# Two kinds of tile for the attention's matmuls, and a reversal done by reads, in a two-layer hybrid block

## The chip, the cores and the metric

The kernel runs on one core of one Trainium2 chip. Its engines are TensorE (PE, with its weight loads as PEld), VectorE (DVE), ScalarE (ACT), GpSimd (POOL) and SyncE (SP), whose queue issues most of the DMA transfers. The metric is device microseconds of one execution.

## What is computed

The reference runs two layers over 256 latent tokens and 256 context tokens of width 1024. A layer is a half-step SwiGLU, then four token mixers side by side (a 31-tap convolution, a gated linear recurrence in both directions, a gated delta net in both directions, and attention with 8 query heads over 2 key heads of width 64), merged through gates, projected, and a second half-step SwiGLU. The second layer computes no context output. Cut to what the change touches:

```python
# attention: keys in the window (latent tokens) and all context keys; a sink per head
s = einsum('bqhgd,bkhd->bhgqk', qg, kk) * 64 ** -0.5        # masked to the band
probs = softmax(concatenate(logits + [sink_col], -1))
out = einsum('bhgqk,bkhd->bqhgd', probs[..., :n], vv)        # the sink's share is dropped
...
# delta net: one direction runs on reversed tokens, its output is reversed back
o = o_forward + flip(o_backward)
y = o * rsqrt(mean(o * o) + eps) * g_norm * silu(z)
```

## The kernel before

All arithmetic is float32. The large matmuls split each operand into two float32r parts (lines 120 and 121 make the parts of a weight, on ACT and on POOL or DVE) and add three products (lines 379 to 381). Tokens lie in four tiles of 128: tiles 0 and 1 are the context, 2 and 3 the latent tokens; the second layer's mixer works on tiles 2 and 3 alone.

The mixer's streams are written as generators, and a hand-written string of letters (ORDER, one for each layer) says in which order their pieces are emitted: "a" is one step of the attention's scores, "b" one of its values, "g" the delta net, "s" its scan, "l" the recurrence, "c" the convolution, "z" gates, "m" merges. A second string (TAIL) orders the delta net's output ("o"), the last merges and the output projection. The framework then schedules the pieces onto the engines by priority, with a timeline of its own estimates (schedule_with_timeline_sim in build), so the order on an engine follows from the dependencies and the free buffers as well as from the letters. SBUF units of 128×512 come from pools (T has 6, G has 8), PSUM banks from three (pm 3, pg 3, px 2).

A step of the attention is one token tile t and one group g: two query heads, one for each key head, stacked on the 128 partitions (64 each). There are 16 steps in the first layer (8 with 256 keys for the context, 8 with 512 for the latent tokens) and 8 of 512 keys in the second. Before, att_z makes two copies of the keys, each with the other head's 64 partitions set to zero (line 1173). att_scores multiplies the stacked queries with each copy over all 128 partitions (line 1210), adds the band's mask by a matmul for latent tokens (line 1213), takes the maximum (line 1214) and the exponential with its sum (line 1221); the sink's exponential, the sum and its reciprocal follow (lines 1223 to 1225). The scores of a context step share one px bank, those of a latent step take two. att_values transposes the unnormalised probabilities (line 1241), copies them back to SBUF (line 1242), multiplies them as stationary operand with 64 columns of values (line 1247), so that tokens lie on the partitions, and scales by the reciprocal (line 1250). After the fourth group the tile is transposed (line 1255), copied (line 1257) and written out (line 1258).

gdn_out, called for four tiles in the first layer and for two in the second, reads a tile of each direction's output from DRAM (line 959) and the gate (line 961), reverses the tokens of the second by a matmul with the matrix J (line 964), which reverses each block of 32, adds both (line 966), squares (line 969), normalises and transposes (line 978). The scan's output lies in DRAM as [pair of chunks, 128, direction, 256], where the 128 are 4 heads by 32 tokens.

Of the kernel before, what the change touches and what calls it, by code (L numbers as in the profile page):

```python
# [17 lines left out]
P = 128  # L18
# [31 lines left out]
class Net:  # L50
# [482 lines left out]
        else:  # L533
            nc.vector.tensor_add(x, x, t1)

# [1 line left out]

    def z_mm(self, ps, w, H, c):
        for k in range(KD):
# [413 lines left out]
    def gdn_out(self, go, y):  # L953
        nc = self.nc
        V = nc.vector
        o1, ot, sz = self.G(), self.G(), self.G()
        tok = slice(go * P, (go + 1) * P)
        for x, d, g in ((o1, 1, (1 - go) if go < 2 else (5 - go)), (ot, 0, go)):
            nc.sync.dma_start(x.rearrange("p (q c) -> p q c", q=2),
                              self.ospill[2 * g:2 * g + 2, :, d].rearrange("q p c -> p q c"))  # L960
        nc.sync.dma_start(sz.rearrange("p (h t) -> p h t", h=4), self.szspill[:, :, tok])
        pj = self.ps("pg")
        for i in range(4):
            nc.tensor.matmul(pj[:, (3 - i) * P:(4 - i) * P], self.gcst("J"), o1[:, i * P:(i + 1) * P],
                             start=True, stop=True)
        V.tensor_add(ot, pj, ot)
        sq = self.small(4, "osq", 1)
        for i in range(4):
            nc.scalar.activation(pj[:, i * P:(i + 1) * P], ot[:, i * P:(i + 1) * P], AF.Square,
                                 accum_out=sq[:, i:i + 1])  # L970
        V.tensor_scalar(sq, sq, 1.0 / 128, 4 * NORM_EPS, op0=ALU.mult, op1=ALU.add)
        rr = self.small(4, "orr", 1)
        nc.gpsimd.tensor_tensor(rr, sq, self.mhalf[:, :4], op=ALU.pow)
        o3 = ot.rearrange("p (n e) -> p n e", n=4)
        V.tensor_mul(o3, o3, rr.unsqueeze(2).to_broadcast([P, 4, P]))
        pt = self.ps("pg")
        for i in range(4):
            nc.tensor.transpose(pt[:, i * P:(i + 1) * P], ot[:, i * P:(i + 1) * P], self.ident)
        p4 = pt.rearrange("p (n h t) -> p n h t", n=4, h=4)
        for h in range(4):  # L980
            y3 = o1[:, h * P:(h + 1) * P].rearrange("p (n t) -> p n t", n=4)
            V.scalar_tensor_tensor(y3, p4[:, :, h], self.vec[:, V_GN:V_GN + 1],
                                   sz[:, h * P:(h + 1) * P].rearrange("p (n t) -> p n t", n=4),
                                   op0=ALU.mult, op1=ALU.mult)
        self.y_part(y, tok, o1.rearrange("p (h t) -> p h t", h=4))
# [152 lines left out]
    def att_z(self, l, H, last):  # L1138
# [24 lines left out]
        def k():  # L1163
            load()
            S["kv"] = self.slot("B", name="kv")
            u = [S["kv"][:, e * 512:(e + 1) * 512] for e in range(4)]
            kf = u[3]
            S["vt"] = u[2]
            rope(self.z(l, Z_AK, H, full), full, kf)
            S["kz"] = []  # L1170
            for i in range(2):
                kk = u[i]
                V.tensor_scalar(kk, kf, S["ac"][:, 896 + i:897 + i], None, op0=ALU.mult)
                S["kz"].append(kk)

        def v():
            pv = self.z(l, Z_AV, H, full)
# [20 lines left out]
    def att_scores(self, S, t, g):  # L1198
# [4 lines left out]
        q = S["q"][:, g * 512 + t * P:g * 512 + (t + 1) * P]  # L1203
        w = (4 if t >= 2 else 2) * P
        mx, den, es = (self.small(2, n, 3) for n in ("mx", "den", "es"))
        ps = [self.ps("px") for _ in range(w // 256)]
        if t < 2:
            ps = [ps[0][:, :w], ps[0][:, w:]]
        for kv in range(2):
            nc.tensor.matmul(ps[kv], q, S["kz"][kv][:, :w], start=True, stop=t < 2)  # L1210
            if t >= 2:
                o = 5 - t
                nc.tensor.matmul(ps[kv][:, o * P:(o + 1) * P], self.ident, band[t - 2], start=False, stop=True)
            V.reduce_max(mx[:, kv:kv + 1], ps[kv], axis=mybir.AxisListType.X)
# [8 lines left out]
        nc.scalar.activation(es, es, AF.Exp)  # L1223
        V.tensor_add(den, den, es)
        V.reciprocal(den, den)
        S["pr"].append((pr, den))

    def att_values(self, S, t, g):
        nc = self.nc
        V = nc.vector  # L1230
        pr, den = S["pr"].pop(0)
        nk = 4 if t >= 2 else 2
        w = nk * P
        if g == 0:
# [6 lines left out]
                nc.tensor.transpose(pt[kv][:, kt * P:(kt + 1) * P], pr[kv][:, kt * P:(kt + 1) * P], self.ident)  # L1241
            nc.scalar.copy(pr[kv], pt[kv])
        po = self.ps("px")
        for kv in range(2):
            o = po[:, 64 * kv:64 * kv + 64]
            for kt in range(nk):
                nc.tensor.matmul(o, pr[kv][:, kt * P:(kt + 1) * P],
                                 S["vt"][:, kt * P + 64 * kv:kt * P + 64 * kv + 64],
                                 start=kt == 0, stop=kt == nk - 1)
        V.tensor_mul(S["ya"][:, g * P:(g + 1) * P].rearrange("p (k e) -> p k e", k=2),  # L1250
                     po[:, :P].rearrange("p (k e) -> p k e", k=2), den.unsqueeze(2).to_broadcast([P, 2, 64]))
        if g == 3:
            pt = self.ps("px")
            for e in range(4):
                nc.tensor.transpose(pt[:, e * P:(e + 1) * P], S["ya"][:, e * P:(e + 1) * P], self.ident)
            yt = self.T()
            nc.scalar.copy(yt, pt)
            nc.sync.dma_start(self.ysp[3][:, :, t * P:(t + 1) * P], yt.rearrange("p (g t) -> p g t", g=4))

    def y_split(self, b, c):  # L1260
        y = self.new_y()
# [297 lines left out]
```

## Time and profile before

| | us |
|---|---|
| median of 3 runs | 2820.98 (2819.75 to 2821.17) |
| span of the profiled execution | 2816.3 |
| the median above that span | 4.7 |
| PE busy | 2593.8 |
| DVE busy | 1955.0 |
| ACT busy | 1093.3 |
| POOL busy | 1008.0 |

The profile is of one execution; its span runs from the first to the last instruction that it shows, and what lies around the span is in the runs' times alone. PE's busy time counts each matmul with its modelled end, so instructions overlap in it; what an instruction costs in a row of them is read from start to start.

### The profile page before, as it was taken

How to read it: one execution, taken by the hardware profiler on the slowest of the kernel's cores; microseconds unless marked ns; L12 is line 12 of the kernel's file. 1: busy time of each engine (PE TensorE's matmuls, PEld its weight loads, DVE VectorE, ACT ScalarE, POOL GpSimd, SP SyncE). 2: the span in 40 equal slices, each digit the busy share in tenths (PEclk: the TensorE clock that was granted, in tenths of full speed). 3: DMA queues.
4: the chain of work that ended last, by engine and by line, in shares of the span. 5: the costliest groups of instructions: out<-in, count | busy, mean ns of one | idle time of the engine just before them, and what ended most of it. 6: DMA issues, size and time to landing. Idle time of an engine off the chain costs nothing.

```text
span 2816.3 us, 37869 instructions
## 1 busy us (share of the span) xinstructions
PE 2593.8 (92%) x14382; PEld 2174.2 (77%) x14382; DVE 1955.0 (69%) x3129; ACT 1093.3 (39%) x1995; POOL 1008.0 (36%) x691
## 2 busy tenths in 40 slices
PE   5999998998898999999999999999979878888898
PEld 3787877776777787878878888888867767688898
DVE  8695966678999834265969467623698898756455
ACT  3322235483332533353222442223536534344443
POOL 4323223222535344433232332323332278731221
PEclk9999999999999999999999999999989989999899
DMA  6554542234422343434545344423222534357353
GB/s 226 191 179 169 201 145 102 69 109 153 140 83 91 113 135 117 164 113 157 181 171 196 102 166 167 149 95 115 91 90 92 156 116 133 105 183 240 135 181 118
DMA packets 162216, 396.99 MB, mean 141 GB/s; under 512 B 28417, under 2 KB 68577, under 8 KB 161265
## 3 DMA queue, kind: packets, MB, share of 16 engines
q1 hardware_dynamic: 158114, 384.55, 40.9%
q10 hardware_dynamic: 3888, 9.96, 1.1%
q8 instruction: 113, 1.85, 0.3%
q14 instruction: 69, 0.57, 0.1%
q0 software_dynamic: 32, 0.07, 0.0%
HBM read 360.92 MB, written 33.60 MB: 140 GB/s over the span
## 4 chain that ended last, share of the span: by engine, by line
PE 34%; DVE 13%; issue 3%; DMA 2%; POOL 2%; ACT 2%; SPq 0%; POOLq 0%; ACTq 0%; DVEq 0%
PE pm L380 10%; PE pm L381 10%; PE pm L379 10%; DVE C L1107 2%; DVE G L572 1%; DVE junk L169 1%; DVE wl L121 1%; DVE G L864 1%; PE px L381 1%; PE px L380 1%; PE px L379 1%; DMA wr<-in_wo_dram 1%; DVE lru L1049 1%; DVE M L781 1%; PE pg L873 0%
## 5 line engine op out<-in xcount | busy, mean ns | idle before, releaser
L379 PE MATMUL pm<-h,wh 128*128 128x512 f32 (+1 forms) x2512 | 895.5, 358 | 36.6 <-ACT h L125 12.8
L381 PE MATMUL pm<-h,wl 128*128 128x512 f32 (+1 forms) x2512 | 890.9, 355 | 16.8 <-DVE wl L121 14.8
L380 PE MATMUL pm<-h,wh 128*128 128x512 f32 (+1 forms) x2512 | 892.0, 355 | 13.0 <-POOL h L127 6.7
L121 POOL TENSOR_TENSOR wl<-wr,wh 128x1024 fp32r<-128x1024 f32 x166 | 419.8, 2530 | 697.6 <-ACT wh L120 649.0
L120 ACT CAST wh<-wr 128x1024 fp32r<-128x1024 f32 x340 | 356.7, 1050 | 785.6 <-PE pm L380 275.2
L379 PEld LDWEIGHTS pm<-h,wh 128*128 128x128 f32 x2512 | 484.0, 193 | 109.1 <-ACT h L125 15.6
L381 PEld LDWEIGHTS pm<-h,wl 128*128 128x128 f32 x2512 | 484.8, 193 | 87.0 <-DVE wl L121 18.8
L380 PEld LDWEIGHTS pm<-h,wh 128*128 128x128 f32 x2512 | 485.1, 193 | 80.9 <-POOL h L127 10.1
L121 DVE TENSOR_TENSOR wl<-wr,wh 128x1024 fp32r<-128x1024 f32 x174 | 243.6, 1400 | 263.0 <-ACT wh L120 261.6
L169 DVE SCALAR_TENSOR_TENSOR junk<-wa,cb 128x1024 bf16<-128x1024 f32 x256 | 358.3, 1442 | 9.2 <-DMA wa<-in_adaw_dram 8.6
L127 POOL TENSOR_TENSOR F<-G,F 128x512 fp32r<-128x512 f32 (+1 forms) x94 | 139.4, 1483 | 426.2 <-ACT F L125 426.1
L1107 DVE SCALAR_TENSOR_TENSOR C<-C,vec 128x482 f32<-128x482 f32 (+29 forms) x240 | 208.2, 867 | 4.1 <-ACT C L1099 0.9
L380 PE MATMUL pm<-wl,F 128*128 128x512 f32 x368 | 145.5, 395 | 0.0
L379 PE MATMUL pm<-wh,F 128*128 128x512 f32 x368 | 145.4, 395 | 0.0
L381 PE MATMUL pm<-wh,F 128*128 128x512 f32 x368 | 144.1, 395 | 0.0
L393 DVE TENSOR_TENSOR G<-G,pm 128x512 f32<-128x512 f32 (+1 forms) x93 | 54.4, 585 | 125.9 <-PE pm L381 118.9
L121 DVE TENSOR_TENSOR wl<-raw,wh 128x1024 fp32r<-128x1024 f32 x61 | 75.0, 1231 | 63.6 <-ACT wh L120 63.6
L125 ACT CAST F<-G 128x512 fp32r<-128x512 f32 (+1 forms) x94 | 50.9, 542 | 154.1 <-DVE G L393 154.1
L868 POOL TENSOR_TENSOR wk<-wk,cd 128x512 f32<-128x512 f32 x56 | 70.8, 1267 | 94.1 <-PE pg L890 75.4
L572 DVE SCALAR_TENSOR_TENSOR G<-pm,vec,G 128x506 f32<-128x506 f32 (+5 forms) x126 | 87.2, 692 | 24.5 <-ACT G L567 22.7
L120 ACT CAST wh<-raw 128x1024 fp32r<-128x1024 f32 x64 | 66.8, 1047 | 88.1 <-PE pm L380 38.8
L1294 POOL TENSOR_TENSOR mrg<-mrg,M 128x512 f32<-128x512 f32 (+1 forms) x48 | 51.9, 1085 | 117.5 <-DVE M L1293 117.5
(408 smaller groups left out, 4493.8 us busy)
## 6 DMA issues: line engine op xcount, KB each, us to landing
wr<-in_f_dram SPq DMA_DIRECT2D x204, 512.0 KB, 3.6
wa<-in_adaw_dram SPq DMA_DIRECT2D x72, 1024.0 KB, 4.9
wr<-in_win_dram SPq DMA_DIRECT2D x132, 512.0 KB, 3.6
raw<-in_f_dram SPq DMA_DIRECT2D x30, 1024.0 KB, 4.9
wr<-in_prj_dram SPq DMA_DIRECT2D x32, 512.0 KB, 3.7
gt<-gsp SPq DMA_DIRECT2D x12, 768.0 KB, 5.2
gsp<-G SPq DMA_DIRECT2D x32, 256.0 KB, 2.7
wr<-in_wo_dram SPq DMA_DIRECT2D x16, 512.0 KB, 3.7
```

Of the source, the lines that this page charges most:

```text
L120: nc.scalar.copy(h, r)
L121: (nc.gpsimd if pool_lo else nc.vector).tensor_sub(l, r, h.bitcast(F32))
L127: eng.tensor_sub(lo, src, hi.bitcast(F32))
L169: nc.vector.scalar_tensor_tensor(junk, w3[:, a], 1.0, self.cb[:, s], op0=ALU.mult, op1=ALU.mult, accum_out=self.modT[l][:, i + a, s:s + 1])
L379: nc.tensor.matmul(ps, wh, xh, start=first, stop=False)
L380: nc.tensor.matmul(ps, wh, xl, start=False, stop=False)
L381: nc.tensor.matmul(ps, wl, xh, start=False, stop=last)
L393: nc.vector.tensor_mul(hf[:, c], sg[:, c], pu[:, c])
L572: nc.vector.scalar_tensor_tensor(acc[:, :, d:], src[:, :, :n - d], w(j), acc[:, :, d:], op0=ALU.mult, op1=ALU.add)
L868: nc.gpsimd.tensor_mul(S(d, n + 1).rearrange("p (h e) -> p h e", h=4), S(d, n).rearrange("p (h e) -> p h e", h=4), gs["cd"][:, d * N_CH + ...
L1107: V.scalar_tensor_tensor(o, x, w(j), o, op0=ALU.mult, op1=ALU.add)
L1294: nc.gpsimd.tensor_add(dst, dst, th[:, c])
```

## The change

The keys are no longer copied and masked. A step's scores are two matmuls, each over the 64 partitions of its own head, into a px bank each, issued one behind the other and before the band's matmuls. The probabilities are normalised on ACT at the end of att_scores. att_values takes the values as stationary operand and the transposed probabilities as moving one, so that the two heads' outputs land on the two halves of the partitions, already transposed; the output transposes, their copy and the scaling go, and a plain copy brings the tile to SBUF. In gdn_out the second direction is read by four transfers that walk each block of 32 tokens backwards; the matmuls with J and their PSUM bank go, and the Squares write their unused result to SBUF.

```diff
     def gdn_out(self, go, y):
-        for x, d, g in ((o1, 1, (1 - go) if go < 2 else (5 - go)), (ot, 0, go)):
-            nc.sync.dma_start(x.rearrange("p (q c) -> p q c", q=2),
-                              self.ospill[2 * g:2 * g + 2, :, d].rearrange("q p c -> p q c"))
+        nc.sync.dma_start(ot.rearrange("p (q c) -> p q c", q=2),
+                          self.ospill[2 * go:2 * go + 2, :, 0].rearrange("q p c -> p q c"))
+        g = (1 - go) if go < 2 else (5 - go)
+        for i in range(4):
+            nc.sync.dma_start(o1[:, i * P:(i + 1) * P],
+                              self.ospill[2 * g + 1 - i // 2, :, 1, (1 - i % 2) * P:(2 - i % 2) * P]
+                              .rearrange("(h t) c -> h t c", h=4)[:, ::-1])
         nc.sync.dma_start(sz.rearrange("p (h t) -> p h t", h=4), self.szspill[:, :, tok])
-        pj = self.ps("pg")
-        for i in range(4):
-            nc.tensor.matmul(pj[:, (3 - i) * P:(4 - i) * P], self.gcst("J"), o1[:, i * P:(i + 1) * P],
-                             start=True, stop=True)
-        V.tensor_add(ot, pj, ot)
+        V.tensor_add(ot, o1, ot)
...
-            nc.scalar.activation(pj[:, i * P:(i + 1) * P], ot[:, i * P:(i + 1) * P], AF.Square,
+            nc.scalar.activation(o1[:, i * P:(i + 1) * P], ot[:, i * P:(i + 1) * P], AF.Square,
...
     def att_z(self, l, H, last):
-            S["kz"] = []
-            for i in range(2):
-                kk = u[i]
-                V.tensor_scalar(kk, kf, S["ac"][:, 896 + i:897 + i], None, op0=ALU.mult)
-                S["kz"].append(kk)
+            S["kf"] = kf
...
     def att_scores(self, S, t, g):
-        ps = [self.ps("px") for _ in range(w // 256)]
-        if t < 2:
-            ps = [ps[0][:, :w], ps[0][:, w:]]
+        ps = [self.ps("px")[:, :w] for _ in range(2)]
         for kv in range(2):
-            nc.tensor.matmul(ps[kv], q, S["kz"][kv][:, :w], start=True, stop=t < 2)
+            e = slice(64 * kv, 64 * kv + 64)
+            nc.tensor.matmul(ps[kv], q[e], S["kf"][e, :w], start=True, stop=t < 2)
+        for kv in range(2):
             if t >= 2:
...
         V.reciprocal(den, den)
-        S["pr"].append((pr, den))
+        for kv in range(2):
+            nc.scalar.activation(pr[kv], pr[kv], AF.Copy, scale=den[:, kv:kv + 1])
+        S["pr"].append(pr)
...
     def att_values(self, S, t, g):
-        for kv in range(2):
-            o = po[:, 64 * kv:64 * kv + 64]
-            for kt in range(nk):
-                nc.tensor.matmul(o, pr[kv][:, kt * P:(kt + 1) * P],
-                                 S["vt"][:, kt * P + 64 * kv:kt * P + 64 * kv + 64],
-                                 start=kt == 0, stop=kt == nk - 1)
-        V.tensor_mul(S["ya"][:, g * P:(g + 1) * P].rearrange("p (k e) -> p k e", k=2),
-                     po[:, :P].rearrange("p (k e) -> p k e", k=2), den.unsqueeze(2).to_broadcast([P, 2, 64]))
+        for kt in range(nk):
+            for kv in range(2):
+                nc.tensor.matmul(po[64 * kv:64 * kv + 64, :P], S["vt"][:, kt * P + 64 * kv:kt * P + 64 * kv + 64],
+                                 pr[kv][:, kt * P:(kt + 1) * P], start=kt == 0, stop=kt == nk - 1)
+        V.tensor_copy(S["ya"][:, g * P:(g + 1) * P], po[:, :P])
         if g == 3:
-            pt = self.ps("px")
-            for e in range(4):
-                nc.tensor.transpose(pt[:, e * P:(e + 1) * P], S["ya"][:, e * P:(e + 1) * P], self.ident)
-            yt = self.T()
-            nc.scalar.copy(yt, pt)
-            nc.sync.dma_start(self.ysp[3][:, :, t * P:(t + 1) * P], yt.rearrange("p (g t) -> p g t", g=4))
+            nc.sync.dma_start(self.ysp[3][:, :, t * P:(t + 1) * P], S["ya"].rearrange("p (g t) -> p g t", g=4))
```

## Rows read from the trace of the kernel before

**Rows 1.** The page, part 1: busy time, share of the span, instructions.

```profile
PE 2593.8 (92%) x14382; PEld 2174.2 (77%) x14382; DVE 1955.0 (69%) x3129; ACT 1093.3 (39%) x1995; POOL 1008.0 (36%) x691
```

**Rows 2.** Busy microseconds by stretch: length, PE, PEld, DVE, ACT, POOL, clock, DMA.

```profile
540.00:680.00 140.00, 128.47 (x718) 108.07 (x717) 109.57 (x252) 85.05 (x289) 32.27 (x17) 0.98 0.38 120
680.00:960.00 280.00, 250.85 (x1658) 196.50 (x1657) 261.85 (x393) 98.37 (x172) 131.56 (x123) 0.95 0.33 106
960.00:1080.00 120.00, 119.91 (x585) 96.77 (x583) 55.60 (x83) 51.81 (x88) 52.02 (x31) 1.00 0.42 136
...
2090.00:2280.00 190.00, 156.68 (x977) 136.38 (x978) 168.43 (x388) 93.44 (x271) 49.38 (x25) 0.90 0.37 117
```

**Rows 3.** Waits of PE, 2090 to 2280 us: total us, times, longest.

```profile
PE px L1241 <- ACT T L1221: 10.0, 3, 5.0
...
PE px L1255 <- DVE T L1250: 3.7, 2, 2.8
```

**Rows 4.** Instruction groups by form, PE: count, busy us, mean ns, idle before.

```profile
L1247 PE MATMUL px<-kv,T 128*128 128x64 f32 x320 | 44.1, 286 | 3.4 <-ACT T L1242 2.2 <-ACT T L1221 1.2
L1210 PE MATMUL px<-kv,q 128*128 128x512 f32 x64 | 35.7, 641 | 9.2 <-DVE T L1250 6.0 <-DVE T L1159 3.1
...
L1210 PE MATMUL px<-kv,q 128*128 128x256 f32 x32 | 10.2, 400 | 0.4 <-DVE mx L1214 0.4
...
L964 PE MATMUL pg<-G,gcst 128*128 128x128 f32 x48 | 6.9, 277 | 0.9 <-DMA G<-ospill 0.9
...
L1255 PE MATMUL px<-ident,T 128*128 128x128 f32 x24 | 4.8, 290 | 3.9 <-DVE T L1250 3.9
```

**Rows 5.** Instruction groups by form, ACT, 540 to 2290 us.

```profile
L1242 ACT COPY T<-px 128x512 f32<-128x512 f32 x32 | 18.3, 598 | 9.8 <-PE px L1241 9.7
...
L1242 ACT COPY T<-px 128x256 f32<-128x256 f32 x16 | 6.2, 388 | 8.6 <-PE px L1241 8.6
```

**Rows 6.** PE in order of time, 749 to 767 us: start, duration, count.

```profile
750.38 0.39 PE L885 MATMUL pg<-vn,G 128*128 128x128 f32 x2
750.69 0.43 PE L890 MATMUL pg<-wk,gt 128*32 128x128 f32 x8
751.05 1.16 PE L833 MATMUL pg<-gt 128*128 128x128 f32 x8
752.04 1.02 PE L1210 MATMUL px<-kv,q 128*128 128x512 f32 x2
752.91 0.38 PE L1213 MATMUL px<-acst,ident 128*128 128x128 f32 x2
...
762.00 1.09 PE L1241 MATMUL px<-ident,T 128*128 128x128 f32 x8
763.03 0.64 PE L854 MATMUL pg<-wk,gt 128*32 128x128 f32 x16
763.60 1.10 PE L1247 MATMUL px<-kv,T 128*128 128x64 f32 x8
764.54 0.44 PE L885 MATMUL pg<-vn,G 128*128 128x128 f32 x2
```

**Rows 7.** PE in order of time, from 713 us.

```profile
713.02 1.89 PE L1247 MATMUL px<-kv,T 128*128 128x64 f32 x16
714.75 1.08 PE L1210 MATMUL px<-kv,q 128*128 128x512 f32 x2
...
717.90 1.02 PE L1210 MATMUL px<-kv,q 128*128 128x512 f32 x2
```

**Rows 8.** All engines in order of time, 705 to 708 us.

```profile
705.53 0.68 ACT L1221 ACTIVATE T<-px,mx 128x512 f32<-128x512 f32 x1
...
707.12 0.15 DVE L1225 RECIPROCAL den<-den 128x2 f32<-128x2 f32 x1
```

**Rows 9.** SP's DMA issues in order of time, from 2482 us.

```profile
2482.78 0.89 SPq L959 DMA_DIRECT2D G<-ospill  x2
...
2486.04 0.62 SPq L104 DMA_DIRECT2D wr<-in_prj_dram  x1
```

More of the change, by code (lines that the diff above doesn't have):

```diff
@@ L1230, in att_values @@
         V = nc.vector
-        pr, den = S["pr"].pop(0)
+        pr = S["pr"].pop(0)
         nk = 4 if t >= 2 else 2
```

## Prediction

> **What bounds the kernel now.** I read the profile's page first, then busy time by stretch around the attention and the delta net's output, then who waits for whom on PE, and last PE, ACT, DVE and SP in order of time at the places that the change touches. On the page PE is busy 92% of the span [rows 1]; the stretches show that this is an average over stages with different limits [rows 2]. The first layer's attention begins at 550 us: up to 680 us PE is busy 92%, DVE 78% and ACT 61%; from 680 to 960 us DVE is the limit, 262 of 280 us, with PE at 90%. From 960 to 1080 us, where the delta net's output is made, PE alone is: 119.9 of 120 us. The second layer's attention (2090 to 2280 us) has DVE at 89% and PE at 82%, and there PE stands idle because of the attention itself: its transposes of the probabilities wait 10.0 us for the exponentials, and the output transposes (line 1255) 3.7 us for the scaled output [rows 3]. So a microsecond taken from PE is worth a whole one at 960 to 1080 us, part of one in the attention, and a longer softmax chain is paid on PE at once where PE has nothing ready in its order.
>
> **The reversal.** Six calls of gdn_out lose four fp32 matmuls each, which the profile records as 48 instructions [rows 4]. A full-array instruction of this kind takes 0.11 us from start to start (sixteen of line 1247 in 1.73 us [rows 7]; line 964's have the same weight load). 48 × 0.11 = 5.3 us of PE, 3.5 in the first layer, where PE is full: −3.4 taken, nearly whole. The second layer's 1.8 us lie behind weight loads: −1.6 at most. Instead of one read of the reversed half there are four, 18 more issues over the kernel. In the first layer SP has room and the reads are early. At the second layer's end six issues (four reads of the scan's output and two of the gate) hold SP from 2482.78 to 2486.04, 0.54 us each, and the load of the projection's weights stands behind them [rows 9]; six more put it 3.3 us later. Whether that reaches the end depends on the buffer that this load fills: 0 to +3.3, I take +1.6, since the chunks before it are still in use, which cancels the −1.6. The sum of DVE now reads two SBUF operands in place of PSUM and SBUF; the Squares write SBUF. I see no price for either and cost both at nothing; an engine with slack there (DVE 55.6 of 120 us [rows 2]) covers a few tenths.
>
> **The scores.** 16 steps of 512 keys and 8 of 256 issue 64 and 32 instructions now [rows 4]; a pair of 512 takes 0.87 us (752.04 to 752.91 [rows 6]), a pair of 256 half that. Run together, the two heads' halves would hide one pair per step. The trace has no row tiles; the nearest are the scan's column tiles of 128×32. From 750.38 to 752.04 us two full instructions, eight tiled and eight full ones take 1.66 us; less ten at 0.11 that leaves 0.56 for the eight tiled. From 762.00 to 764.54 sixteen full and sixteen tiled ones take 2.54; less 1.73 that leaves 0.81 for sixteen [rows 6]. So eight more cost 0.25, or 0.03 each instead of 0.11: the tiles do run together. The rest, 0.31 us, is there however few they are: the price of one visit to the tiled mode. Both heads must then be adjacent on PE. Here the second head waits for the second px bank, which the previous step's output holds: 714.75 and 717.90 [rows 7]. Of the 16 long steps only 3 have the two heads in one place; in the short ones both share a bank, so the second follows the first's reduce. If nothing changes in this, 21 separate steps pay two visits, 21 × 0.62 = +13.0, and three gain 0.87 − 0.31: +11.3 in all. If all pair: 16 × −0.56 + 8 × −0.12 = −9.9. The new order issues both before the band's matmuls and gives the short steps two banks, so some will pair: I take the middle, +0.7.
>
> The Trainium skill, "TensorEngine Tiling (Array Packing)", section "Theoretical Speedup", puts up to a factor of two on a dimension of 64 or less; its section "Key Properties" says that a change of tiling mode drains the engine. The rows above agree with both, and 0.31 us is the drain's price here. By the factor alone the scores would give back 17 us of PE and the values 17, which is the third case below.
>
> **The values.** Sixteen instructions of 64 columns take 1.73 us now, bound by their weight loads. Afterwards eight packed pairs of 128 columns take 8 × 0.11 + 0.31 = 1.19: −0.54 per long step, −0.12 per short one (0.87 to 0.75), −9.6 for 24 steps. But the 320 instructions stand in 37 groups, not 24 (counted on PE in order of time; one step's eight at 763.60 is half of a long one [rows 6]); each extra group costs 0.31: +4.0. Net −5.6, bounds −9.6 and 0.
>
> **The output transposes** go: 24 instructions, 2.6 us, their wait of 3.7 us [rows 3, 4], and six ACT copies. Some of that wait will find another ending, so −4.0, bounds −6.3 and −2.0.
>
> **The normalising** adds two ACT copies per step. The nearest rows are the copies of the transposed probabilities, 0.60 us for 512 and 0.39 for 256 [rows 5]: 32 × 0.60 + 16 × 0.39 = 25 us, less 3.6 for six copies of the same length. ACT is idle 39% or more in these stretches [rows 2], so most is covered; in the first stretch, where a 39% reserve meets chains through ACT, I take +1, bounds 0 and +5. What matters more is where they stand. Today the transposes may start when the exponential is done; the sum's reciprocal runs beside them and is needed only at the end. Afterwards the exponential of the sink, DVE's add and reciprocal and the scaling lie ahead of the first transpose. At 705 us the exponential ends at 706.21 and the reciprocal at 707.27 [rows 8]: 1.06, plus 0.60 for the first scaling, is 1.7 us later, with DVE's queue as it was there. Behind the transposes on PE stand the weights' matmuls. On ACT, behind the scaling, stand the casts of the next weights (line 120), for which PE's large matmuls wait. Three transposes of the second layer wait for the exponential now [rows 3]; with 1.7 us more each that is +5.1, and if all 24 steps were exposed, +41. Most steps have other work ahead in PE's order, and the order is drawn up anew for the changed dependencies, so I take +3, bounds 0 and +41.
>
> **Smaller.** Four masked copies of the keys go, 0.5 us of DVE each, ahead of the DVE-bound stretch: −0.5 of 2. The copy that replaces the scaling of the output is about as long. The short steps take a second px bank but lose the wait of the second head for the first's reduce: nothing taken, ±2.
>
> **The sum.** Scores and values together are −4.9 of PE; where DVE is at 78 to 94% half of it counts, −2.4. With −3.4 (reversal), 0 (its second layer), −4.0, +1, +3 and −0.5 that is −6.3. The span of 2816.3 becomes 2810.0; the median of the runs shown lies 4.7 above that span, so 2814.7, rounded to 2815.
>
> **The rivals.** A bound for no change is 0.2%, 5.6 us: about what a measurement of this kernel can tell from none.
> 1. Small gain, as summed: 2807 to 2815. For it: the reversal and the output transposes are certain, on an engine that is full or waiting there. Chance 0.32.
> 2. The gains cancel, 2816 to 2826, about 2820: heads stay apart, so that tiling costs 5.7 of PE instead of gaining 4.9 (+2.9 in place of −2.4, −1.0 in all), or DVE's 262 of 280 us hides the rest. Chance 0.28.
> 3. Full packing: heads pair, groups stay whole. Scores −9.9, values −9.6, two thirds of it kept, 13 instead of 2.4, transposes −6.3, chain 0: −22, or 2799. By the Trainium skill's factor, without a price for the drain (34 us), it would be an estimate of about 2790. Against it: 13 of 16 long steps have their heads microseconds apart. Chance 0.13.
> 4. Slower: the scaling stands on PE's path. Each exposed step costs 1.7 us. Without the chain's term the sum is −9.3, so from the sixth exposed step the change loses, from the ninth it is slower by over 0.2%, and with sixteen it comes to +18, 2839. For it: real DVE queues are longer than the instruction durations, and the transposes already wait in three places of the second layer. Against it: the scores run one or two steps ahead of the values. Chance 0.27.
>
> Faster: rivals 1 and 3, 0.45; within 0.2%: 0.28; slower: 0.27. The range reaches from full packing to fourteen exposed steps (2821 − 9.3 + 24): 2798 to 2836. The first case's own range is 2807 to 2815.
>
> **What would show it.** Line 964 and line 1255 are gone. At 960 to 1080 us PE's work is 3 us less and the later stages start earlier by as much. The tiled forms 64×128 and 128×64 appear; two heads' scores start within 0.2 us of each other if they pair, and the next full instruction then comes 1.2 us after the first of a long step. PE's wait for the scaled probabilities replaces its wait for the exponential: under 15 us in all if I am right, over 25 for rival 4. ACT is 21 us busier. The prediction is wrong if the new order of the engines moves the conv and scan work against each other, which no row of before can show, or if the reversed read lands much later than the 64 KB reads of other tiles.

## The result, and the profile after

The change makes the kernel slower: 2843.24 us (median; 2835.27 to 2855.49) against 2820.36 for the kernel before on the same chip, a ratio of 1.0079 with a 95% interval of 1.0052 to 1.0106, or 22 us. Forecast were 2815, with 2798 to 2836 as the range. The profiled execution took 2841.13 us, its span 2839.1.

The page's part 1 after (it answers to [rows 1]):

```profile
PE 2608.2 (92%) x14310; PEld 2153.4 (76%) x14310; DVE 1937.2 (68%) x3125; ACT 1114.4 (39%) x2037; POOL 1019.5 (36%) x691
```

PE executes 72 instructions fewer and is busy 14.4 us longer; ACT is 21 us busier, as forecast. Busy time by stretch after, the same stretches as [rows 2] (length, PE, PEld, DVE, ACT, POOL, clock, DMA), and below them the stretch in which most is lost:

```profile
540.00:680.00 140.00, 123.23 (x656) 96.18 (x654) 104.03 (x238) 83.88 (x289) 28.98 (x15) 0.95 0.38 117
680.00:960.00 280.00, 252.09 (x1614) 187.81 (x1614) 240.66 (x370) 109.41 (x193) 134.25 (x122) 0.93 0.31 99
960.00:1080.00 120.00, 111.72 (x543) 86.51 (x542) 64.18 (x95) 45.46 (x87) 49.42 (x30) 0.99 0.42 132
2090.00:2280.00 190.00, 160.99 (x1015) 129.64 (x1014) 161.27 (x362) 102.03 (x283) 53.00 (x27) 0.91 0.37 115
...
545.00:1240.00 695.00, 637.39 (x3460) 492.25 (x3459) 460.94 (x754) 293.88 (x642) 280.64 (x205) 0.96 0.37 118
```

The same stretch of before:

```profile
545.00:1240.00 695.00, 652.36 (x3630) 525.76 (x3629) 490.48 (x804) 293.92 (x638) 280.34 (x211) 0.98 0.37 120
```

The first reading: between 545 and 1240 us PE stands idle 57.6 us in place of 42.6, at a granted clock of 0.96 in place of 0.98, and has done 170 instructions less at the end (48 of them are matmuls with J and output transposes, which the change took out of this stretch). The stretch from 960 to 1080 us, where PE was full [rows 2], has a hole of 8.3 us.

Where the time goes is found by following one thing through both traces: the start of the same matmul after, less its start before. Where the engines' orders agree this lag is constant; where it steps, something was lost. For the change it is -5.6 us at 545 us (nothing has changed by then; single executions drift by some us there), +21.2 at 1180, +22.1 at 2060 and +22.5 at 2800. So the whole loss lies between 545 and 1180 us, the first layer's attention, delta net, conv and scan; the second layer's attention costs nothing. One execution can stray by much of such a lag: in rev_pool_old_order (below), which between 597 and 797 us does before's work in before's order, the lag rises from -4.2 to +6.2 us there, at a granted clock of 0.93 in place of 0.97. So a step of a lag says something only where a wait beside it explains it.

The single instructions did what the prediction said. Instruction groups by form, PE and ACT, after (they answer to [rows 4, 5]):

```profile
L1244 PE MATMUL px<-T,kv 128*64 128x128 f32 x320 | 32.0, 289 | 5.7 <-ACT T L1240 5.5
L1205 PE MATMUL px<-kv,q 64*128 64x512 f32 x64 | 38.8, 688 | 5.4 <-DVE T L1159 3.6 <-DVE T L1246 1.9
...
L1239 PE MATMUL px<-ident,T 128*128 128x128 f32 x160 | 26.1, 290 | 17.8 <-ACT T L1223 11.6 <-ACT T L1217 4.3 <-ACT T L1240 2.0
...
L1223 ACT ACTIVATE T<-T,den 128x512 f32<-128x512 f32 x32 | 21.5, 728 | 22.0 <-DVE den L1221 22.0
```

The values' matmuls take 32.0 us where they took 44.1. Over the whole kernel PE waits 11.6 us for scaled probabilities (L1223) and 4.3 for exponentials (L1217); before it waited 10.7 for exponentials. Under 15 was the mark set for the prediction, so by that mark rival 4 is not the cause. But 10.0 of before's 10.7 us lie in the second layer [rows 3], where nothing was lost; the waits of the stretch that loses stand below. PE in order of time after, from 817 us (it answers to [rows 6, 7]):

```profile
817.92 1.09 PE L1244 MATMUL px<-T,kv 128*64 128x128 f32 x16
818.94 1.12 PE L1205 MATMUL px<-kv,q 64*128 64x512 f32 x2
820.00 0.49 PE L1209 MATMUL px<-acst,ident 128*128 128x128 f32 x2
```

A long step's values take 1.02 us to the next instruction (1.73 before, 1.19 forecast). A head's scores, alone between other work, take 1.06 (0.87 before). The two heads follow one another in PE's order in only 3 of 24 steps, and in two of these the second head still comes over a microsecond after the first; they run together in one, a short step at 555.76 us.

PE's waits after, 545 to 1240 us (total us, times, longest):

```profile
PE pg L873 <- DVE vn L858: 11.8, 6, 4.3
PE pg L885 <- DVE G L893: 7.3, 4, 4.8
PE px L1239 <- ACT T L1217: 4.3, 3, 2.0
PE px L1239 <- ACT T L1223: 4.0, 1, 4.0
...
PE pg L854 <- DVE wk L877: 0.5, 1, 0.5
```

and before:

```profile
PE pg L854 <- DVE wk L877: 6.7, 4, 4.3
PE pg L873 <- DVE vn L858: 5.7, 3, 2.7
PE pg L885 <- DVE G L893: 4.9, 2, 3.2
...
PE px L1241 <- ACT T L1221: 0.7, 2, 0.5
```

Two things grew. The delta net's waits at L873 and L885 are 8.5 us longer, that at L854 6.2 shorter; all waits on the delta net's banks (pg) together went from 23.8 to 30.7 us. And the transposes of the probabilities, which waited 0.7 us for ACT's exponentials, now wait 8.3 for exponentials and scaled probabilities; all waits of the attention's own matmuls went from 7.7 to 14.2 us. These two, +6.9 and +6.5, make most of the 15 us of added idle time.

The short steps also take longer. The last one's scores and the first of 512 keys, before:

```profile
632.94 0.60 PE L1210 MATMUL px<-kv,q 128*128 128x256 f32 x2
...
643.75 1.02 PE L1210 MATMUL px<-kv,q 128*128 128x512 f32 x2
```

After, the last short step's scores stand at 671.40 us and the first of 512 keys at 678.37, although the first short step begins 5.5 us earlier (544.67 in place of 550.21).

One place shows how a short wait grows. PE in order of time after, 675 to 689 us (in brackets the idle time ahead, and what ended it):

```profile
675.42 0.44 PE L1239 MATMUL px<-ident,T 128*128 128x128 f32 x2 [1.98 <-ACT T L1217]
676.38 0.44 PE L1239 MATMUL px<-ident,T 128*128 128x128 f32 x2 [0.52 <-ACT T L1240]
677.78 0.65 PE L1244 MATMUL px<-T,kv 128*64 128x128 f32 x6 [0.61 <-ACT T L1240]
678.37 2.07 PE L1205 MATMUL px<-kv,q 64*128 64x512 f32 x2
680.37 0.79 PE L1209 MATMUL px<-acst,ident 128*128 128x128 f32 x2
681.09 2.07 PE L1205 MATMUL px<-kv,q 64*128 64x512 f32 x2
```

The window from 680 to 690 us (columns as in the table of stretches):

```profile
680.00:690.00 10.00, 7.70 (x16) 4.26 (x16) 6.73 (x22) 4.39 (x11) 1.53 (x2) 0.50 0.25 72
```

After these waits (1.98, 0.52 and 0.61 us) the granted clock is 0.50 (the lower level, 1.2 GHz), scores take 2.00 us in place of 1.06, and the large matmuls of the projections stand 0.43 us apart until 691.7, 0.23 from there. Over the stretch from 545 to 1240 us, 0.96 in place of 0.98 is, as an estimate from the two levels, 28 us more at half the clock, worth up to 13 us (28 × 0.20 / 0.43, by the large matmuls here).

### The profile page after: what moved, and what is told of

It reads as the page before. It is cut to its first block, busy times and chain, and to the rows that moved or that the text cites. A ratio compares the mean times of both kernels' runs of the same rounds, so it can differ in the third digit from the quotient of the medians.

```text
span 2839.1 us, 37810 instructions
## 1 busy us (share of the span) xinstructions
PE 2608.2 (92%) x14310; PEld 2153.4 (76%) x14310; DVE 1937.2 (68%) x3125; ACT 1114.4 (39%) x2037; POOL 1019.5 (36%) x691
## 4 chain that ended last, share of the span: by engine, by line
PE 40%; DVE 10%; issue 2%; ACT 2%; DMA 1%; POOL 1%; SPq 0%; POOLq 0%; ACTq 0%; DVEq 0%
PE pm L380 11%; PE pm L381 11%; PE pm L379 11%; DVE C L1107 3%; DVE G L572 1%; PE pg L873 1%; PE px L381 1%; PE px L379 1%; PE px L380 1%; DVE G L864 1%; DVE lru L1049 1%; DVE M L781 0%; POOL h L127 0%; DVE cv L610 0%; DMA wr<-in_wo_dram 0%
## 5 line engine op out<-in xcount | busy, mean ns | idle before, releaser
L121 POOL TENSOR_TENSOR wl<-wr,wh 128x1024 fp32r<-128x1024 f32 x166 | 424.1, 2556 | 705.5 <-ACT wh L120 640.0
L120 ACT CAST wh<-wr 128x1024 fp32r<-128x1024 f32 x340 | 356.7, 1050 | 787.2 <-PE pm L380 272.3
L121 DVE TENSOR_TENSOR wl<-wr,wh 128x1024 fp32r<-128x1024 f32 x174 | 242.8, 1395 | 267.4 <-ACT wh L120 265.7
L121 DVE TENSOR_TENSOR wl<-raw,wh 128x1024 fp32r<-128x1024 f32 x61 | 74.8, 1228 | 62.6 <-ACT wh L120 62.4
L868 POOL TENSOR_TENSOR wk<-wk,cd 128x512 f32<-128x512 f32 x56 | 69.2, 1240 | 108.2 <-PE pg L890 77.5
L120 ACT CAST wh<-raw 128x1024 fp32r<-128x1024 f32 x64 | 66.8, 1047 | 86.5 <-PE pm L380 37.7
```

Of the source, the lines that this page charges most:

```text
L120: nc.scalar.copy(h, r)
L121: (nc.gpsimd if pool_lo else nc.vector).tensor_sub(l, r, h.bitcast(F32))
L868: nc.gpsimd.tensor_mul(S(d, n + 1).rearrange("p (h e) -> p h e", h=4), S(d, n).rearrange("p (h e) -> p h e", h=4), gs["cd"][:, d * N_CH + ...
```

## The experiments

A ratio is that of a kernel's runs to those of the kernel before on the same chip, with its 95% interval; "us" after it is the ratio times 2821. Theories named in the expectations: A, the longer softmax chain; B, visits to the tiled mode; C, any edit makes the scheduler draw up a new order of all engines, and that costs it; D, the reversed reads and their issues.

**Each part alone, order drawn up freely.**

```
rev_only:  the diff of gdn_out alone
rows_only: the diffs of att_z and att_scores (the scores) alone
norm_only: the scaling of pr in att_scores; values and output as before, without the den
cols_only: norm_only and the new att_values
```

> The kernel before with the reversal by reads alone. Theory A (the longer softmax chain costs the time): this part gains about 3 us, 2817 to 2818. Theory B (row-tiled scores with their heads apart cost it): the same, 2817 to 2818. Theory C (any edit redraws the order of the engines, and the order costs it): a move that the work removed (5 us of PE) does not explain, of more than 8 us either way. Theory D (the four reads or their issues are late): slower, by up to 20 us.

> The kernel before with the scores as two row tiles alone: no masked keys, a bank for each head, both matmuls ahead of the mask's. A: within 6 us of before. B: slower by 11 us or more, with 0.3 us on each of some 40 visits and the granted clock lower in the attention. C: a move that the visits do not explain. D: no change.

> The kernel before with the probabilities normalised on ScalarE ahead of their transposes; values, output transposes and reversal as before, with a plain copy of the output. A: slower by most of the change's loss, 15 to 25 us, with TensorE waiting for the scaled probabilities. B and D: at most 5 us slower. C: any move of more than 8 us without such waits.

> The kernel before with normalised probabilities and the values as two column tiles, without the output transposes; scores and reversal as before. A: slower by 5 to 20 us, since the packed values and the transposes give back 6 to 16 us of what the chain costs. B and D: faster by 4 to 8 us. C: no relation to the run with the normalising alone.

Measured: rev_only 1.0061 (1.0037 to 1.0085), 17 us; rows_only 1.0157 (1.0132 to 1.0181), 44; norm_only 1.0066 (1.0046 to 1.0087), 19; cols_only 1.0043 (1.0024 to 1.0062), 12. Every part alone loses, and together they lose less than rows_only by itself. norm_only's 19 us lie where A put them, but without A's waits: PE's transposes wait 0.6 us for scaled probabilities between 545 and 1240 us, 0.7 before for exponentials, so C fits. A cannot be all of it: rev_only doesn't touch the attention. In rev_only PE waits, 955 to 1120 us:

```profile
PE pm L379 <- ACT wh L120: 8.5, 4, 5.4
PE px L1124 <- DMA T<-cspill: 3.6, 1, 3.6
```

The first was 0.2 us before. Without the J matmuls the scheduler moves the sum's Squares forward in ACT's order; at 965.25 us ACT waits 4.83 us there for the sum, which waits 3.96 us for the reads, and the casts of the next weights (L120) stand behind.

**The same work in an equal order.** To take the order out, later kernels carry the order of another kernel: each listed instruction gets an edge without a wait to the one that stood before it on its engine.

```diff
-    Net(ctx, tc, t, out).run()
+    Net(ctx, tc, t, out).run(); chain(tc)
...
+def chain(tc):
+    info = mybir.DependencyInfo(mybir.DependencyClass.NoSync, mybir.DependencyReason.DATA)
...
+        for a, b in zip(at, at[1:]):
+            tc.add_manual_dep(on[b], on[a].name, info, reason="order")
```

> The reversal alone (four J matmuls per call gone, five reads instead of two), but PE, DVE and ACT are told to take their instructions in exactly the order of the kernel before; only SP's extra reads stand anew. Theory C (the engines' new order costs it): the 17 us that the reversal alone lost are gone, and what is left is the work: between 5 us less and 2 us more than before. Theory D (the extra issues on SP or the late reversed reads): the reads are as many and as late, so it stays 10 us or more above before.

> The row-tiled scores alone, with PE in before's order except for the scores themselves, and DVE and ACT in before's order outside the attention. Theory C: most of the 44 us that the rows alone lost are gone; what stays is the price of the tiling visits, between 0 and 12 us above before. Theory B (visits to the tiled mode, the px banks, the clock): these are as many as with the free order, so it stays 30 us or more above before.

> The kernel before, no operation changed, but PE (except the scores), DVE and ACT (outside the attention) take their instructions in the order which the rows alone had. Theory C: the order by itself costs it, 25 us or more above before. Theory B: without tiling there is nothing to lose; within 6 us of before.

> The whole change, with PE in before's order except for the scores (its transposes and value matmuls stand where they stood), and DVE and ACT in before's order outside the attention. Theory C: the 22 us are gone and the sum of the prediction shows, 2 to 8 us under before. Theory A (the longer softmax chain): the transposes stand where they were while the scaled probabilities come 1.7 us later, so PE waits in most steps, and it is 15 us or more above before. B and D: 15 us or more above, too.

Measured: rev_old_order 1.0013 (0.9999 to 1.0027), 4 us; rows_old_order 1.0130 (1.0088 to 1.0172), 37; before_rows_order 1.0104 (1.0081 to 1.0127), 29; after_old_order 1.0120 (1.0096 to 1.0143), 34. Two findings. The kernel before, with not one operation changed, loses 29 us in rows_only's order, and 13 of rev_only's 17 us go when the old order is put back: an order by itself can cost as much as the whole change lost. That the change's own order costs that isn't shown: no run put before's work into it. And an order held for work that it was not drawn up for can overcharge: the second bank below costs 36 us in before's order and 17 in one of its own. The stretch of before_rows_order, to be held against 652.36 and 0.98:

```profile
545.00:1240.00 695.00, 640.02 (x3520) 514.37 (x3520) 459.65 (x756) 284.65 (x616) 275.75 (x205) 0.96 0.38 118
```

But the old order doesn't save the rows or the whole: C is not all. The lag of rows_old_order rises by 32 us between 550 and 640 us, where the eight steps of 256 keys stand, and by 4 more from there to 2060.

**One cause each.** The second px bank of the short steps became theory E. two_banks is the kernel before with

```diff
-        ps = [self.ps("px") for _ in range(w // 256)]
-        if t < 2:
-            ps = [ps[0][:, :w], ps[0][:, w:]]
+        ps = [self.ps("px")[:, :w] for _ in range(2)]
```

long_rows_old_order has row tiles in the long steps alone, cols_old_order is cols_only and att_long_old_order both, all in before's order.

> The kernel before, with one thing changed: a step of 256 keys takes two px banks for its two heads' scores instead of one (no row tiles, the same matmuls). Theory E (new: px has two banks, and the eight short steps of the first layer, 550 to 640 us, can no longer overlap with one another): 10 us or more above before, lost before 700 us. Rival (the second bank costs nothing, as the prediction took it): within 6 us of before.

> Row-tiled scores in the steps of 512 keys alone, the short steps as before in one bank; PE, DVE and ACT in exactly the order of the kernel before. What differs is the tiling itself. Theory E and the order (C): 0 to 6 us above before (32 lone matmuls at 0.19 us more each are 6 at most). Theory B (visits to the tiled mode cost it): 20 us or more above before.

> Normalised probabilities and column-tiled values, scores as before; PE in exactly the order of before, DVE and ACT in it outside the attention. Theory C: the work's own gain shows, 2 to 9 us under before (5.6 of the values and 4.0 of the output transposes, less the chain). Theory A (the longer softmax chain, rival 4 of the prediction): the transposes stand where they stood and PE waits in most steps for the scaled probabilities; 10 us or more above before.

> The attention's part of the change with row tiles in the long steps alone (short steps keep one bank), without the reversal, in before's order as in the run beside it. Theories C and E: the sum of the two runs beside it, 8 us under to 4 us above before. Theory A: 10 us or more above.

Measured: two_banks 1.0060 (1.0044 to 1.0076), 17 us, most of it (14) before 740 us; long_rows_old_order 1.0064 (1.0042 to 1.0085), 18; cols_old_order 1.0041 (1.0026 to 1.0055), 12; att_long_old_order 1.0057 (1.0038 to 1.0077), 16. In long_rows_old_order and att_long_old_order I had written both heads' scores of a short step ahead of both maxima, in one bank, and the first maximum came to wait for the second scores (6.6 us at one place in the first of them); that is undone below. The losses don't add up: 18 and 12 us stand together at 16. cols_old_order loses in the attention, by the chain. ACT and DVE there, in order of time:

```profile
554.17 0.15 DVE L1224 TENSOR_TENSOR den<-den,es 128x2 f32<-128x2 f32 x1
554.29 0.75 DVE L572 SCALAR_TENSOR_TENSOR G<-pm,vec,G 128x510 f32<-128x510 f32 x1
554.95 0.15 DVE L1225 RECIPROCAL den<-den 128x2 f32<-128x2 f32 x1
556.34 0.73 ACT L608 ACTIVATE G<-G 128x512 f32<-128x512 f32 x1
556.86 0.79 ACT L567 ACTIVATE G<-pm,vec 128x512 f32<-128x512 f32 x1
557.43 1.01 ACT L1227 ACTIVATE T<-T,den 128x256 f32<-128x256 f32 x2
```

The exponentials are done at 553.5; the reciprocal stands behind a conv instruction on DVE, the scaling behind twelve exponentials of the decay (L698) and two conv instructions on ACT. PE's transposes wait 4.9 us for it, where I had 1.7.

> Row-tiled scores in the steps of 512 keys alone, the short steps untouched; all five engines in exactly the order of the kernel before. (In the run of the long rows before this, the first head's maximum in the short steps had come to wait for the second head's scores, since both were written before it in one bank; that is undone here.) Only the tiling differs. Theory B as the prediction priced it: 32 lone matmuls at 0.19 us more each, 2 to 6 us above before. Rival (each visit costs more than the matmul's own time): 12 us or more above.

> The kernel before with two px banks for a short step's scores, no row tiles; PE in before's order except for the scores, DVE and ACT in it outside the attention. Theory E (a short step that needs both banks cannot start before the step ahead of it has let go of its last): 20 us or more above before, lost between 550 and 640 us, on PE waiting for the exponentials. Rival (in the bank's own run it was the new order that cost it): within 8 us of before.

> The reversal alone, its four reads issued by POOL instead of SP; PE, DVE and ACT in before's order. Theory D in its narrow form (the reads hold up SP, behind which the conv's read and the projection's weights stand: 3.5 us at 1080 us and 3.5 us at 2495 us): those two waits are gone and the matmuls' 3 us are gained, 1 to 5 us under before. Rival (the reversed reads themselves land late): 2 us or more above before, PE or DVE waiting for ospill.

> Column-tiled values from the unnormalised probabilities: the reciprocals are spread over the partitions by two more column-tiled matmuls per step and multiplied in at the end (one ACT copy more of 128 columns, no output transposes). PE, DVE and ACT in before's order, the new matmuls and copies free. Theory A (of the 12 us that the column tiles lost in the old order, the chain through the reciprocal and the scaling is the cause): between 5 us under and 4 us above before, no wait of the transposes longer than before's. Rival (the column tiles themselves cost it): 8 us or more above.

Their edits, besides the held order: long_rows_same_order writes the short steps as before; two_banks_old_order is two_banks; rev_pool_old_order has `nc.gpsimd.dma_start` for the four reversed reads; late_norm_old_order has column tiles without the scaling:

```diff
+        for kv in range(2):
+            nc.tensor.matmul(po[64 * kv:64 * kv + 64, P:2 * P], den[:, kv:kv + 1].to_broadcast([P, 64]), self.ident,
+                             start=True, stop=True)
+        ya = S["ya"][:, g * P:(g + 1) * P]
+        nc.scalar.copy(ya, po[:, :P])
+        V.tensor_mul(ya, ya, po[:, P:2 * P])
```

Measured: long_rows_same_order 1.0023 (1.0007 to 1.0038), 6 us; two_banks_old_order 1.0129 (1.0112 to 1.0146), 36; rev_pool_old_order 1.0013 (0.9998 to 1.0029), 4; late_norm_old_order 1.0009 (0.9997 to 1.0021), 3.

The tiling costs what its instructions cost: 32 lone scores at 0.19 us more each are 6.1. The second bank, at an equal order, costs as much as rows_old_order lost, without a single tile. PE's waits in two_banks_old_order, 550 to 680 us:

```profile
PE px L1241 <- ACT T L1221: 22.0, 7, 4.8
PE px L1210 <- ACT T L1221: 2.9, 1, 2.9
```

Before, that first wait is 0.2 us there. PE in order of time, two_banks_old_order:

```profile
585.27 1.03 PE L1210 MATMUL px<-kv,q 128*128 128x256 f32 x4
589.41 0.44 PE L1241 MATMUL px<-ident,T 128*128 128x128 f32 x2 [3.11 <-ACT T L1221]
```

and before:

```profile
581.94 0.60 PE L1210 MATMUL px<-kv,q 128*128 128x256 f32 x2
582.38 0.38 PE L1241 MATMUL px<-ident,T 128*128 128x128 f32 x2
583.47 0.60 PE L1210 MATMUL px<-kv,q 128*128 128x256 f32 x2
583.90 0.38 PE L1241 MATMUL px<-ident,T 128*128 128x128 f32 x2
```

px has two banks. With one for a short step's scores, the transposes of the step ahead, which need a bank too, run between the scores of its two heads. With two, the scores hold the whole of px, and the transposes behind them, still those of the step ahead, wait for a bank until the exponentials have read the scores. In two_banks_old_order the exponential of the first head ends at 589.26 us and its sum is read at 589.36; the transposes start at 589.41:

```profile
588.79 0.47 ACT L1221 ACTIVATE T<-px,mx 128x256 f32<-128x256 f32 x1 [2.47 <-DVE mx L1215]
589.17 0.19 ACT L1221 ACTIVATION_READ_ACCUMULATOR T<-px,mx 128x1 f32 x1
```

The same form stands in the change at 675.42 us, where transposes, whose own input is the scaled probabilities, wait 1.98 us for exponentials (L1217).

Where two heads do come together, the row tiles run together. A step of 512 keys in rows_old_order, at a granted clock of 1.00 (all instructions have a helper's line there):

```profile
2159.87 1.13 PE L1567 MATMUL px<-kv,q 64*128 64x512 f32 x4
2160.93 0.71 PE L1567 MATMUL px<-acst,ident 128*128 128x128 f32 x4
```

Both heads take 1.06 us to the next instruction, as much as one alone in the change; the same pair takes 1.74 in full-array form [rows 6].

late_norm_old_order lost 9 us less than cols_old_order: most of that loss is the chain's, though each of the two ratios is known to some 4 us only. The other half of its expectation missed: its transposes wait longer than before's (longest 6.0 us, before 5.0).

The narrow form of D falls: with the reads off SP's queue the loss is the same. The lag steps down at each call's place in the first layer, by 0.45, 0.44, 0.45 and 0.90 us, then up by 3.3 where PE waits:

```profile
PE px L1124 <- DMA T<-cspill: 3.9, 1, 3.9
```

Transfers in rev_pool_old_order, 960 to 1100 us (KB each, median us from issue to landing); before, the 256 KB reads of ospill took 3.6 and those of cspill 4.0:

```profile
G<-ospill POOLq DMA_DIRECT2D x16, 64.0 KB, 5.2
G<-ospill SPq DMA_DIRECT2D x4, 256.0 KB, 6.7
T<-cspill SPq DMA_DIRECT2D x4, 256.0 KB, 4.8
```

Two things make up the 3.3 us at the cspill read that PE waits for. It takes 5.3 us from issue to landing in place of 4.0. And it is issued at 1080.31 us in place of 1076.47, 1.9 us later than the lag just ahead of it (1.95) accounts for: in SP's queue a load of weights stands before it that waits for DVE's cast (L121) to end, at 1079.90 in place of 1076.06. So slower transfers beside the reads are part of the price; why the cast ends later stays open.

The last two runs asked how the parts add up. after_one_bank is the whole change with the short steps' scores as before. rest_old_order was to be the change without the second bank and without the chain in before's order; the kernel that ran under this name did not carry the held order, so its engines' orders are freely drawn, and its expectation is to be read so.

> The whole change, but the steps of 256 keys keep their old scores (masked keys, one px bank); the engines' order drawn up freely, as for the change itself. Theory E (the second bank of the short steps is a main part of the 22 us): 10 us or less above before. Rival (a free order finds its way round the second bank, and the chain and the rest make the 22): 15 us or more above before.

> The whole change with both main suspects undone (short steps in one bank; values column-tiled from unnormalised probabilities, the reciprocals multiplied in at the end), PE, DVE and ACT in before's order. What is left is row tiles in the long steps, column tiles and the reversal, which alone cost 6.0, 2.5 and 3.7 us at an equal order. If the parts add up: 9 to 15 us above before, against 35 for the whole change in that order. If something else in the whole costs it: 20 us or more above.

Measured: both 1.0125 (1.0102 to 1.0149), 35 us. What is left in rest_old_order costs 6 + 3 + 4 = 13 us at before's order, if the three runs alone add up, and 35 at its own; no run has the three together at before's order. after_one_bank, with one loss taken out of the change, is 13 us slower than the change. Theory E's expectation of 10 us or less failed, and the rival's number held: in a free order the second bank's price can't be read off the whole.

## Why the prediction was wrong

Two steps of the prediction failed. One is the second px bank, "nothing taken, ±2": at an equal order it costs 36 us. The other is the sum itself, which prices each edit in the order of before and has no term for a new order, though the prediction names it last among what would prove it wrong: "The prediction is wrong if the new order of the engines moves the conv and scan work against each other, which no row of before can show". No version whose order was drawn up anew stayed within 10 us of before (seven edits beside the change: 12, 17, 17, 19, 35, 35 and 44 us slower), and before's own work in a foreign order lost 29. How much of the order changes differs: compared as sequences of operation, names and shape, PE's instructions of rev_only and two_banks are 98% those of before, those of the change 81%. In the change, PE's added 15 us of idle time lie in the first layer's stretch, about half on the delta net's waits for DVE and ACT (+6.9) and half on the attention's own (+6.5), and the lower clock adds to it. Which of them comes from the order, which from the second bank and which from the chain isn't shown.

By the prediction's own steps, at an equal order:

- **The reversal**, -3.4 in the first layer and 0 in the second. The matmuls gave back 2.2 us of the 3.4; the wait for cspill, which the prediction doesn't have, took 3.3. At the second layer's end the issues before the projection's weights were bounded at +3.3; in rev_old_order that load is issued 3.3 us later and the lag rises by 2.9 from there to the end. Net +4 (0 to +8), mis-sized at both ends.
- **The scores**, +0.7 within -9.9 and +11.3: the long steps cost +6, by the mechanism given, since almost nothing pairs. The price of a visit was mis-sized: a lone head's scores cost 0.19 us more, where 0.31 was taken. A pair, where one came, saves 0.68 us (1.74 less 1.06), where 0.56 was taken.
- **"The short steps take a second px bank but lose the wait of the second head for the first's reduce: nothing taken, ±2."** 36 us at an equal order. I looked at what the second head gains, not at which other instructions live in px: the transposes need a bank of it. How much of it the change's own order pays stays open: three waits of this form show (4.3 us, 1.98 of them among the short steps), and the first step of 512 keys begins 35 us later than before (two_banks, which has the bank alone, and after_one_bank, which lacks it, begin theirs at 681 and 644 us), but other work fills much of that time.
- **The values**: 1.02 us per long step, 1.19 forecast, and the output transposes gone: the instructions' price is right. That the saving reaches the kernel's time isn't shown. late_norm_old_order has both gains, with two matmuls and an ACT copy more in each step, and is 3 us slower (-1 to +6), where the two terms were -2.8 (half of the -5.6) and -4.0.
- **The normalising**, +3 with 1.7 us per exposed step: 12 less 3 is 9 at an equal order. The chain's price is not its instructions but the queues in which its links stand.
- **The rivals**: 4 named the right direction, and its mechanism is there in part: in the stretch that loses, the transposes' waits for ACT grew from 0.7 to 8.3 us, of which 4.0 are for scaled probabilities, once, while the other 4.3 have the form of the bank's. That it named the direction is in part luck, since neither the order nor the bank is in it. Full packing needs heads that run together. The Trainium skill, "TensorEngine Tiling (Array Packing)", section "Theoretical Speedup", gives up to a factor of two for a dimension of 64 or less; the runs agree where it applies, with 1.64 for the pair of heads above (1.74 to 1.06 us) and 1.70 for a long step's values (1.73 to 1.02 us), changes of mode included.

What stays open is the split of the 22 us. Each edit made to separate its parts draws a new order, which by itself moves the time by more than the parts. Two rivals have no run: before's work in the change's own order, and the change with letters in ORDER and TAIL written for it, since those that it has were written for the kernel before. No version was faster than the kernel before; late_norm_old_order and rev_old_order can't be told from it.

## What to carry to other kernels

Where a scheduler draws up the order, an edit is two changes; hold the order to price the work, knowing that an order drawn up for other work can overcharge, and run the old work in the new order to price the order. In a kernel at 92% of its bound engine, expect a new draw to cost more than small savings bring. Before giving a step a second buffer, list who else needs that pool between its fill and its release; before putting one more link into a chain, look at what stands in the queues where it must wait.

## What the runs showed of the hardware

- A lone fp32 row tile of 64 rows takes longer than the full array's matmul of the same columns: 1.06 us for 512 columns from start to start in place of 0.87 [rows 6], at a granted clock of 1.00 both times (817 to 821 us after, 750 to 754 us before).
- Two such tiles on the two halves of the array's rows run together when they stand next to each other: 1.06 us for both in place of 1.74 for two full-array matmuls (rows_old_order, 2159.87 us, granted clock 1.00).
- In the change, PE's waits of 1.98, 0.52 and 0.61 us between 675 and 678 us were followed by a stretch at half the clock (0.50 at 680 to 690 us). By the instructions shown there it cost more than these waits, an estimate of 2 × 0.94 us on scores and 10 × 0.20 on large matmuls, 3.9 us against 3.1.
- Beside four reversed reads of 64 KB, the 256 KB reads of the same tensor took 6.7 us (four of them, 2.8 to 10.5, POOL issuing the reversed ones) in place of 4.2 before (eight, 2.7 to 6.0), 950 to 1100 us. With so few and such a spread this is a tendency, not a price.
